# A second buffer for gathered expert rows, other groups of routed blocks, and one weight buffer less

## The chip, the cores and the metric

The kernel runs on one core of a Trainium2 chip. The metric is the device time of one execution in microseconds. TensorE is called PE here, its weight loads PEld, VectorE DVE, ScalarE ACT, GpSimd POOL and SyncE SP, as in the profile; SP only issues DMAs.

## What is computed

One layer of a decoder trunk on 1024 tokens of width 1024: a mixer (three kinds of token mixing side by side and one output projection), then a mixture of 32 experts, of which each token uses two, and a last RMSNorm.

```python
x = x + g_m * hybrid_mixer(h, w_in, ..., w_out)
h = rms_norm(x, norm_ffn_g) * (1.0 + sc_f) + sh_f
p_g = softmax(h @ w_rg + b_rg)                 # 4 groups, the best one is taken
e_logits = (h @ w_re + b_re)[chosen group]     # 8 experts in it, the best two
hid = silu(xb @ w_gate[e]) * (xb @ w_up[e])    # per expert, on the rows sent to it
out = out + (hid @ w_down[e]) * weight         # back to the tokens' rows
return rms_norm(x + g_f * out, final_norm_g)
```

## The kernel before

Tokens lie in 8 blocks of 128. The mixer ends in `c_steps(b, ...)`, block by block: eight groups of three products of `w_out` for each half of the columns (`ps_wo`, L990 to L992; each fp32 operand is split into a high and a low part, hence three), the residual sum `xb` on DVE (L996), its squares on ACT, and its store to `x1_d`. What follows for block b is spread between the products of block b+1: `post_steps` turns `xb` on PE (`ps_x1t`), multiplies it by the router's weights (`ps_rt`, L1016), writes the logits `L[:, b]` (L1021, L1022), and makes `h2`, the normalised rows that the experts read, which are stored to `h2_d` (L1033). For blocks 0 to 6 `h2` is one multiplication on DVE (L1025) and an addition of `shf` that DVE and POOL share (L1028), and ACT issues the store. For block 7 a multiplication by `af` (L1011) stands early on DVE, ACT multiplies by the row's factor (L1031), POOL adds `shf` (L1032) and SP issues the store.

`route_steps(b0, b1)` works on the logits of several blocks at once, as `RB` says: blocks 0 to 3 behind block 3, 4 to 6 behind block 6, and 7 alone at the end. It picks group and experts on DVE by some 30 small instructions, counts positions with PE (`ps_pos`, L1109 to L1112), and puts the token numbers and the weights into tables of 128 rows by 32 experts with PE (`ps_tab`, L1130 and L1166), two products a block each. The last group's table, `toki` (L1138), tells which 128 rows each expert takes.

The experts run one after another. `gather(e)` (L1306) is an indirect DMA from POOL's queue that reads the rows of expert e from `h2_d` into the one buffer `xg`. `xpose(e)` turns them on PE (`ps_xg`, L1316), eight transposes of 128 by 128 into two PSUM banks, and splits them into `xh` and `xl`. `next_tokens(e)` calls `xpose(e)` and then `gather(e + 1)`, inside the second product of the expert before. Then come the gate and up products (`ps_gu`, L1338 to L1340), the hidden rows, and the down products (`ps_d`), whose weighted result is added to `x1_d` by an indirect DMA from POOL (L1376, called the scatter).

An expert's weights are 6 MB, loaded by SP in halves of 1 MB (`load_half`, L1197) into a ring of `NHALF` = 19 buffers, made of whatever room the mixer leaves free as it ends: `w0`, the pair of `xq0` and the room of `gm` (`wg`), `xq1`, `cy`, and at last the room of `w_out`'s parts (`wx`). Sixteen of them are loaded ahead; the last `POST` = 3 wait until three small memsets on POOL (L1383), which stand behind the first gather, have run. A load may be issued when the load `DC` = 2 places ahead of it has landed, for the first `NC_` = 12, and `DEPTH` = 5 places ahead after that. ACT copies each piece of weights to the high part (`phi`, L1326), DVE subtracts to get the low part (`plo`, same line).

A scheduler sets each engine's order when the program is built, by its own estimates of time; at run time each engine works in that order and waits where data or room is missing. POOL's indirect DMAs stand in POOL's order like its instructions. At the end the last expert's rows are handled apart, with `xr`, which reuses `xg`.

Of the kernel before, what the change touches and what calls it, by code (L numbers as in the profile page):

```python
# [29 lines left out]
DE = 512  # L30
NOV = 15
NSSD = 2
NHALF = 19
SB = 3
XK, HK = 1, 3
WARM = 25
# [6 lines left out]
CP = 11  # L43
AN = 4
QD = 1
DC, NC_ = 2, 12
KORD = (4, 5, 6, 7, 0, 1, 2, 3)
RATE = 1.8
ZW = 2
# [1 line left out]
DEPTH = 5  # L51
NEG = -1.0e30

RB = {3: (0, 4), 6: (4, 7), 7: (7, 8)}


C_BSH, C_BSC, C_NMG = 0, 8, 16
# [17 lines left out]
def mixer_moe(ctx, tc, x, pch, prow, ada_m, ada_r, w_col, w_z, w_v, w_dtf, w_out, w_rt, w_gu, w_dn, out):  # L75
# [902 lines left out]
    def c_steps(b, yh, yl, xbs):  # L978
        bs = slice(b * P, (b + 1) * P)
        xb = xin[b]  # L980
        xT = sc3.tile([P, KT, P], F32, tag="xT", name="xT")
        s2 = sc.tile([P, 4], F32, tag="s2", name="s2")
        h2 = sc3.tile([P, D], F32, tag="h2", name="h2")
        for q in range(2):
            qs_ = slice(512 * q, 512 * (q + 1))
            ps = bank("ps_wo", "pj")
            for n, kt in enumerate(KORD):
                hi, lo = (woc[k][q][:, kt] for k in ("hi", "lo"))
                h_, l_ = (y[:, kt // 4, kt % 4] for y in (yh, yl))
                PE.matmul(ps, h_, hi, start=(n == 0), stop=False)  # L990
                PE.matmul(ps, l_, hi, start=False, stop=False)
                PE.matmul(ps, h_, lo, start=False, stop=(n == KT - 1))  # L992
                if q and n == 5:
                    turn(xb, xT, 0)
                yield
            V.tensor_tensor(xb[:, qs_], ps, xb[:, qs_], op=ALU.add)  # L996
            S.activation(ps, xb[:, qs_], AF.Square, accum_out=s2[:, q:q + 1])
        s1 = S.dma_start(x1_d[bs, :], xb)
        if b == XB:
            room(xsp.tile([P, 4096], F32, name="w0"), s1.ins)  # L1000
            room_of(xqs[0], woc["gmp"].tile([P, D], F32, tag="gm", name="wg"), after=s1.ins)
            room_of(xqs[1], xqs[2], xqs_both, after=s1.ins)
        xbs.append((xb, xT, s2, h2))

    def post_steps(b, xb, xT, s2, h2):
        bs = slice(b * P, (b + 1) * P)
        turn(xb, xT, 1)
        V.tensor_tensor(s2[:, 2:3], s2[:, 0:1], s2[:, 1:2], op=ALU.add)
        rstd_of(s2[:, 3:4], s2[:, 2:3], D, sc, 1)
        if b == NB - 1:  # L1010
            tc.keep_in_program_order(V.tensor_tensor(h2, xb, ccn["af"], op=ALU.mult))  # L1011
        yield
        yield
        pr = bank("ps_rt")
        for kt in range(KT):
            PE.matmul(pr[64 * (kt % 2):64 * (kt % 2) + 64, 0:P], ccn["wrp"][:, kt], xT[:, kt], start=(kt < 2), stop=(kt >= KT - 2))  # L1016
        rT = sc3.tile([P, P], F32, tag="rT", name="rT")
        rc = S.copy(rT, pr[:, 0:P])
        yield
        PE.transpose(pr[:, P:2 * P], rT, ident)  # L1020
        V.scalar_tensor_tensor(L[:, b], pr[:, P:P + 36], s2[:, 3:4], ccn["rbias"], op0=ALU.mult, op1=ALU.add)  # L1021
        V.scalar_tensor_tensor(L[:, b], pr[:, P + 64:P + 100], s2[:, 3:4], L[:, b], op0=ALU.mult, op1=ALU.add)  # L1022
        yield
        if b < NB - 1:
            V.scalar_tensor_tensor(h2, xb, s2[:, 3:4], ccn["af"], op0=ALU.mult, op1=ALU.mult)  # L1025
            for q in range(2):
                hs = slice(512 * q, 512 * (q + 1))
                (V if q else G).tensor_tensor(h2[:, hs], h2[:, hs], ccn["shf"][:, hs], op=ALU.add)  # L1028
        else:
            with tc.issue_after(rc.ins):  # L1030
                S.mul(h2, h2, s2[:, 3:4])  # L1031
            G.tensor_tensor(h2, h2, ccn["shf"], op=ALU.add)  # L1032
        (S if b < NB - 1 else nc.sync).dma_start(h2_d[bs, :], h2)  # L1033
        if b + 2 < NB:
            load_x1(b + 2, S)

# [188 lines left out]
    for b in range(NB):  # L1225
        c = b + NSSD
        ssd = ssd_steps(c, yns, **cst) if c < NB else iter(())
        if c >= NB and ew is None:
# [1 line left out]
            ew = ews.enter_context(tc.tile_pool(name="ew", bufs=1, side="right", reuse_waits="tile"))  # L1230
            room(ew.tile([P, 4096], F32, name="w1"))
            room(ew.tile([P, 2048], F32, name="w2"))
            xg = ew.tile([P, D], F32, name="xg")
            G.memset(xg, 0.0)
        yh, yl = nxt
        for n, _ in enumerate(c_steps(b, yh, yl, xbs)):
            next(ssd, None)
# [65 lines left out]

    with tc.tile_pool(name="ex", bufs=2, reuse_waits="tile") as ex:
        def gather(e):
            return G.indirect_dma_start(xg[:, :], None, h2_d[:, :],  # L1306
                                 bass.IndirectOffsetOnAxis(ap=toki[:, e:e + 1], axis=0),
                                 bounds_check=T - 1, oob_is_err=False)

        def xpose(e):  # L1310
            xh = ex.tile([P, KT, P], F32R, tag="xh", name="xh", bufs=1)
            xl = ex.tile([P, KT, P], F32R, tag="xl", name="xl", bufs=1)
            for q in range(2):
                pt = bank("ps_xg")
                for j in range(4):
                    PE.transpose(pt[:, j * P:(j + 1) * P], xg[:, (4 * q + j) * P:(4 * q + j + 1) * P], ident)  # L1316
                split(xh[:, 4 * q:4 * q + 4], xl[:, 4 * q:4 * q + 4], pt.rearrange("p (j c) -> p j c", c=P))
            return xh, xl

# [61 lines left out]
        with tc.issue_after(g1.ins):  # L1381
            for h in halves[NHALF - POST:]:
                G.memset(h[0][:, 0:1], 0.0)  # L1383
        for _ in range(POST):
            load_half()

# [12 lines left out]
        def next_tokens(e):  # L1399
            if e < NE:  # L1400
                xt.append(xpose(e))
                if e + 1 < NE:
                    gather(e + 1)

        xt, hts = [], []
        next_tokens(0)
# [34 lines left out]
        xbs = free[4:]  # L1441
        for b in LORD:
            nc.sync.dma_start(xbs[b], x1_d[b * P:(b + 1) * P, :])
        xr, XE = xg, G
        rows_of = bass.IndirectOffsetOnAxis(ap=toki[:, NE - 1:NE], axis=0)
        nf = FB * P
        G.indirect_dma_start(xr[:, :], None, x1_d[0:nf, :], rows_of, bounds_check=nf - 1, oob_is_err=False)
# [188 lines left out]
```

## Time and profile before

| what | us |
|---|---|
| median of three runs | 1296.21 |
| lowest and highest of them | 1293.31, 1296.91 |
| the profiled execution | 1301.8 |
| its span, first to last instruction | 1299.9 |
| PE busy | 1202.9 (93%) |
| DVE busy | 976.7 (75%) |
| ACT busy | 738.4 (57%) |
| POOL busy | 270.6 (21%) |

All stages and durations below are those of the profiled execution, whose time lies 5.6 us above the median. The mixer reaches from 0 to about 640 us of its span, the experts from about 655 to 1265, and the last norm ends it. Busy shares are averages over stages with different limits, so they are read for one stage at a time. A row of the order of time has the start, the duration, engine, line, operation, what is written and read, and in brackets the engine's idle time before it and what ended it.

### The profile page before, as it was taken

To read this page: it belongs to the slowest core of one execution; us is meant where nothing else is said; L and a number is where in the kernel's file an instruction comes from. 1 tells how busy PE (TensorE), PEld (TensorE's weight loads), DVE (VectorE), ACT (ScalarE), POOL (GpSimd) and SP (SyncE) were. 2 spreads that over 40 slices of the span, in tenths; PEclk is the share of its full clock that TensorE was granted. 3 is DMA by queue.
4 is the path that set the end of the run, shared out by engine and by line. 5 is a ranking of instruction groups with operands and counts; after the bars stand their busy time and mean duration, and the time that the engine had idled before them with its cause. 6 is when DMAs were issued, how large, how long until landed. Compare 5 with 4: busy or idle time off the path is not lost. (4 is left out here: it accounts for less than half of the span.)

```text
span 1299.9 us, 17279 instructions
## 1 busy us (share of the span) xinstructions
PE 1202.9 (93%) x6079; PEld 930.8 (72%) x6079; DVE 976.7 (75%) x1384; ACT 738.4 (57%) x1146; POOL 270.6 (21%) x200
## 2 busy tenths in 40 slices
PE   5999989999999879999789899999999999999993
PEld 4676646867677558778577677778777877787772
DVE  4789961145265676565678888999999999999985
ACT  4323312233354656653257676777777777787763
POOL 3110302300100253432112222221222122211113
PEclk9999989999999979999879999999999999999997
DMA  9315658642301453734979999999999999999726
GB/s 360 131 42 162 205 166 270 165 114 68 110 17 45 138 171 98 272 109 171 363 267 328 322 321 336 329 364 366 362 359 368 358 364 363 370 359 377 244 53 251
DMA packets 94635, 313.21 MB, mean 241 GB/s; under 512 B 24038, under 2 KB 34454, under 8 KB 73424
## 3 DMA queue, kind: packets, MB, share of 16 engines
q1 hardware_dynamic: 62190, 256.77, 54.3%
q10 hardware_dynamic: 14098, 31.99, 7.2%
q0 software_dynamic: 18256, 23.30, 7.2%
q8 instruction: 49, 0.80, 0.2%
q14 instruction: 42, 0.34, 0.1%
HBM read 289.22 MB, written 39.88 MB: 253 GB/s over the span
## 5 line engine op out<-in xcount | busy, mean ns | idle before, releaser
L1340 PE MATMUL ps_gu<-plo,xh 128*128 128x512 f32 x512 | 209.8, 410 | 7.9 <-DVE plo L1326 7.9
L1338 PE MATMUL ps_gu<-phi,xh 128*128 128x512 f32 x512 | 204.6, 400 | 0.0
L1339 PE MATMUL ps_gu<-phi,xl 128*128 128x512 f32 x512 | 201.8, 394 | 0.6 <-DVE xl L128 0.6
L1326 ACT CAST phi<-wx 128x1024 fp32r<-128x1024 f32 x160 | 167.4, 1053 | 61.6 <-PE ps_gu L1339 55.1
L1326 DVE TENSOR_TENSOR plo<-wx,phi 128x1024 fp32r<-128x1024 f32 x160 | 191.4, 1221 | 14.1 <-ACT phi L1326 9.9
L1376 POOL DMA_INDIRECT x_d<-early,toki x31 | 76.2, 2457 | 378.8 <-DVE early L1372 374.7
L1326 DVE TENSOR_TENSOR plo<-w,phi 128x1024 fp32r<-128x1024 f32 x104 | 125.2, 1221 | 10.8 <-ACT phi L1326 7.9
L1326 ACT CAST phi<-w 128x1024 fp32r<-128x1024 f32 x104 | 108.6, 1052 | 37.3 <-PE ps_gu L1339 32.9
L1340 PEld LDWEIGHTS ps_gu<-plo,xh 128*128 128x128 f32 x512 | 97.1, 190 | 38.0 <-DVE plo L1326 18.5
L1339 PEld LDWEIGHTS ps_gu<-phi,xl 128*128 128x128 f32 x512 | 97.3, 190 | 21.1 <-DVE xl L128 1.4
L1338 PEld LDWEIGHTS ps_gu<-phi,xh 128*128 128x128 f32 x512 | 97.2, 190 | 18.9 <-ACT xh L127 0.4
L1366 PE MATMUL ps_d<-phi,hh 128*128 128x512 f32 x256 | 100.8, 395 | 0.7 <-ACT hh L127 0.7
L1367 PE MATMUL ps_d<-phi,hl 128*128 128x512 f32 x256 | 100.4, 392 | 0.0
L1368 PE MATMUL ps_d<-plo,hh 128*128 128x512 f32 x256 | 96.6, 392 | 0.0
L182 PE MATMUL ps_pr<-h_hi,whi 128*128 128x512 f32 x224 | 91.7, 409 | 0.0
L184 PE MATMUL ps_pr<-h_hi,wlo 128*128 128x512 f32 x224 | 89.2, 398 | 1.3 <-POOL wlo L128 1.3
L183 PE MATMUL ps_pr<-h_lo,whi 128*128 128x512 f32 x224 | 89.3, 398 | 0.0
L223 DVE SCALAR_TENSOR_TENSOR cy<-u_t,cmw,cy 128x1024 f32<-128x1024 f32 x60 | 86.8, 1446 | 2.3 <-ACT cy L220 1.4
L128 POOL TENSOR_TENSOR wlo<-wraw,whi 128x1024 fp32r<-128x1024 f32 x14 | 38.3, 2748 | 178.8 <-ACT whi L127 124.6
L1306 POOL DMA_INDIRECT xg<-h_d,toki x32 | 38.6, 1208 | 109.1 <-PE ps_xg L1316 94.3
L990 PE MATMUL ps_wo<-wo_hi,yh 128*128 128x512 f32 x128 | 55.0, 432 | 1.5 <-ACT yh L127 1.5
L1366 PEld LDWEIGHTS ps_d<-phi,hh 128*128 128x128 f32 x256 | 48.3, 189 | 10.8 <-ACT hh L127 0.9
(403 smaller groups left out, 2629.4 us busy)
## 6 DMA issues: line engine op xcount, KB each, us to landing
wx<-in_w_gu_dram SPq DMA_DIRECT2D x53, 1024.0 KB, 11.6
w<-in_w_gu_dram SPq DMA_DIRECT2D x31, 1024.0 KB, 9.9
wx<-in_w_dn_dram SPq DMA_DIRECT2D x24, 1024.0 KB, 11.7
w<-in_w_dn_dram SPq DMA_DIRECT2D x19, 1024.0 KB, 10.9
at<-in_ada_r_dram ACTq DMA_DIRECT2D x64, 256.0 KB, 4.8
cy<-in_w_gu_dram SPq DMA_DIRECT2D x14, 1024.0 KB, 5.3
wy<-in_w_gu_dram SPq DMA_DIRECT2D x28, 512.0 KB, 13.8
wraw<-in_w_col_dram SPq DMA_DIRECT2D x16, 512.0 KB, 6.0
```

The source lines that it names most:

```text
L182: PE.matmul(ps, hi[:, kt, :], h_hi[hf][:, kt, :], start=(kt == 0), stop=False)
L183: PE.matmul(ps, hi[:, kt, :], h_lo[hf][:, kt, :], start=False, stop=False)
L184: PE.matmul(ps, lo[:, kt, :], h_hi[hf][:, kt, :], start=False, stop=(kt == KT - 1))
L223: yield lambda t=t, k=k: V.scalar_tensor_tensor(cy[:, :, t], v128(u_t[:, t, k:k + T]), cmw[:, t, k:k + 1], cy[:, :, t], op0=ALU.mult, op1= ...
L1326: last[:] = [S.copy(hi, raw).ins, V.tensor_tensor(lo, raw, hi.bitcast(F32), op=ALU.subtract).ins]
L1338: PE.matmul(ps, xh[:, kt], hi[:, ks], start=(kt == 0), stop=False)
L1339: PE.matmul(ps, xl[:, kt], hi[:, ks], start=False, stop=False)
L1340: PE.matmul(ps, xh[:, kt], lo[:, ks], start=False, stop=(kt == KT - 1))
L1366: PE.matmul(pd[n], hh[:, f], hi[:, ns], start=(f == 0), stop=False)
L1367: PE.matmul(pd[n], hl[:, f], hi[:, ns], start=False, stop=False)
L1368: PE.matmul(pd[n], hh[:, f], lo[:, ns], start=False, stop=(f == 3))
L1376: G.indirect_dma_start(x1_d[:, :], bass.IndirectOffsetOnAxis(ap=toki[:, e:e + 1], axis=0), yo[:, :], None, bounds_check=T - 1, oob_is_err= ...
```

## The change

`xq0` becomes the second buffer for gathered rows: `xgs` holds `xg` and `xq0`, expert e uses `xgs[e % 2]`, and both are set to zero once. `gather(1)` is issued right behind the three memsets, and `next_tokens(e)` issues `gather(e + 2)` where it issued `gather(e + 1)`. The pair of `xq0` and the room of `gm` leaves the ring of weight buffers, which has 18 halves then, 15 of them loaded ahead, all 15 two at a time. The routed groups are blocks 0 to 3, 4 and 5, and 6 and 7. The last block's `h2` gets its factor and `shf` in one DVE instruction, and ACT issues its store.

```diff
-NHALF = 19
+NHALF = 18
-DC, NC_ = 2, 12
+DC, NC_ = 2, 15
-RB = {3: (0, 4), 6: (4, 7), 7: (7, 8)}
+RB = {3: (0, 4), 5: (4, 6), 7: (6, 8)}
...
             room(xsp.tile([P, 4096], F32, name="w0"), s1.ins)
-            room_of(xqs[0], woc["gmp"].tile([P, D], F32, tag="gm", name="wg"), after=s1.ins)
             room_of(xqs[1], xqs[2], xqs_both, after=s1.ins)
...
-            with tc.issue_after(rc.ins):
-                S.mul(h2, h2, s2[:, 3:4])
-            G.tensor_tensor(h2, h2, ccn["shf"], op=ALU.add)
-        (S if b < NB - 1 else nc.sync).dma_start(h2_d[bs, :], h2)
+            V.scalar_tensor_tensor(h2, h2, s2[:, 3:4], ccn["shf"], op0=ALU.mult, op1=ALU.add)
+        S.dma_start(h2_d[bs, :], h2)
...
-            xg = ew.tile([P, D], F32, name="xg")
-            G.memset(xg, 0.0)
+            xgs = [ew.tile([P, D], F32, name="xg"), xqs[0]]
+            for xg in xgs:
+                G.memset(xg, 0.0)
...
-            return G.indirect_dma_start(xg[:, :], None, h2_d[:, :],
+            return G.indirect_dma_start(xgs[e % 2][:, :], None, h2_d[:, :],
...
-                    PE.transpose(pt[:, j * P:(j + 1) * P], xg[:, (4 * q + j) * P:(4 * q + j + 1) * P], ident)
+                    PE.transpose(pt[:, j * P:(j + 1) * P], xgs[e % 2][:, (4 * q + j) * P:(4 * q + j + 1) * P], ident)
...
                 G.memset(h[0][:, 0:1], 0.0)
+        gather(1)
...
                 xt.append(xpose(e))
-                if e + 1 < NE:
-                    gather(e + 1)
+                if e + 2 < NE:
+                    gather(e + 2)
...
-        xr, XE = xg, G
+        xr, XE = xgs[0], G
```

The program's order at the end of the mixer, on PE: `ps_x1t` and `ps_rt` are the turned rows and the router's products of block 7, `ps_tab` the tables. Before, from the last products of `w_out` on:

```order
L1130 MATMUL ps_tab<-rEv_5532,rph_5530 128x32
L973 MATMUL ps_x1t<-ident,xb 128x128 x8
L1016 MATMUL ps_rt<-xT,wrp 64x128 x3
L1130 MATMUL ps_tab<-rEv_5542,rph_5540 128x32
...
L1016 MATMUL ps_rt<-xT,wrp 64x128
L1166 MATMUL ps_tab<-roh_5513,rph_5530 128x32
...
L1016 MATMUL ps_rt<-xT,wrp 64x128 x4
L1020 MATMUL ps_rt<-ident,rT 128x128
```

And the same place in the changed program:

```order
L992 MATMUL ps_wo<-wo_lo_3558,yh 128x512
L973 MATMUL ps_x1t<-ident,xb 128x128 x4
L1015 MATMUL ps_rt<-xT,wrp 64x128 x8
L1019 MATMUL ps_rt<-ident,rT 128x128
L1106 MATMUL ps_pos<-rohr,tri_ltr 128x64
```

The tables of the group before the last have left this place; they stand among the products of `w_out` for block 7 now.

The first expert on PE, `ps_gu` being its first gate product. Before:

```order
L1316 MATMUL ps_xg<-ident,xg 128x128 x8
L1338 MATMUL ps_gu<-phi,xh 128x512
L1339 MATMUL ps_gu<-phi,xl 128x512
L1340 MATMUL ps_gu<-plo,xh 128x512
L1338 MATMUL ps_gu<-phi,xh 128x512
```

Changed, with `xq_3931` the second buffer:

```order
L1314 MATMUL ps_xg<-ident,xg 128x128 x8
L1314 MATMUL ps_xg<-ident,xq_3931 128x128 x2
L1336 MATMUL ps_gu<-phi,xh 128x512
L1314 MATMUL ps_xg<-ident,xq_3931 128x128 x5
L1337 MATMUL ps_gu<-phi,xl 128x512
```

Two transposes of expert 1's rows stand ahead of expert 0's first product now, five more right behind it.

POOL's order from the first gather on (`h_d` is `h2_d`, `x_d` is `x1_d`). Before:

```order
L1306 DMA xg<-h_d,toki 128x1024
L1383 MEMSET wx 128x1 x2
L1383 MEMSET wy 128x1
L1306 DMA xg<-h_d,toki 128x1024 x3
L1376 DMA x_d<-early,toki 1024x1024
L1306 DMA xg<-h_d,toki 128x1024
```

Changed:

```order
L1304 DMA xg<-h_d,toki 128x1024
L1381 MEMSET wx 128x1 x2
L1381 MEMSET wy 128x1
L1304 DMA xq_3931<-h_d,toki 128x1024
L1304 DMA xg<-h_d,toki 128x1024
L1304 DMA xq_3931<-h_d,toki 128x1024
L1304 DMA xg<-h_d,toki 128x1024
L1374 DMA x_d<-early,toki 1024x1024
L1304 DMA xq_3931<-h_d,toki 128x1024
```

Five gathers stand ahead of the first scatter instead of four, into the two buffers in turn.

## Rows read from the trace of the kernel before

**Rows 1.** Stretches of the expert stage: length, busy time by engine, clock, DMA share, GB/s.

```profile
700.00:800.00 100.00, 90.76 (x423) 74.19 (x422) 88.86 (x90) 71.80 (x80) 21.16 (x10) 0.98 0.93 327
900.00:1200.00 300.00, 294.59 (x1366) 238.39 (x1365) 288.86 (x294) 231.78 (x262) 55.10 (x32) 1.00 0.99 365
655.00:1226.00 571.00, 549.83 (x2536) 445.36 (x2535) 532.29 (x544) 428.88 (x482) 108.64 (x65) 0.99 0.96 348
```

**Rows 2.** Order of time on POOL, three of the scatters (L1376).

```profile
694.96 3.47 POOL L1376 DMA_INDIRECT x_d<-early,toki  x1 [3.07 <-DVE early L1372]
...
818.54 2.32 POOL L1376 DMA_INDIRECT x_d<-early,toki  x1 [14.18 <-DVE early L1372]
...
1206.27 2.32 POOL L1376 DMA_INDIRECT x_d<-early,toki  x1 [14.70 <-DVE early L1372]
```

**Rows 3.** PE's waits in 660 to 830 us: total, times, longest.

```profile
PE ps_xg L1316 <- DMA xg<-h_d,toki: 12.2, 5, 3.3
```

**Rows 4.** Gathers: two in 653 to 662, seven in 670 to 800, 21 in 820 to 1200.

```profile
DMA to landing us min/median/max: 4.4/6.2/8.0
...
DMA to landing us min/median/max: 5.3/8.0/9.2
...
DMA to landing us min/median/max: 8.4/12.2/13.7
```

**Rows 5.** Two stretches behind waits; columns as in rows 1.

```profile
759.00:763.00 4.00, 3.76 (x12) 3.18 (x13) 1.51 (x3) 1.04 (x1) 0.95 (x1) 0.57 1.00 329
799.00:805.00 6.00, 5.80 (x23) 4.74 (x24) 2.23 (x2) 2.04 (x2) 1.28 (x1) 0.72 0.91 304
```

**Rows 6.** PE's waits in 830 to 1210 us.

```profile
PE ps_gu L1340 <- DVE plo L1326: 7.1, 21, 0.4
```

**Rows 7.** Order of time from the last products of `w_out` to the first gate product.

```profile
622.82 1.28 DVE L1025 SCALAR_TENSOR_TENSOR h<-xb,s,af 128x1024 f32<-128x1024 f32 x1 [0.67 <-POOL s L124]
...
632.53 0.40 PE L992 MATMUL ps_wo<-wo_lo,yh 128*128 128x512 f32 x1
...
633.65 0.47 PE L990 MATMUL ps_wo<-wo_hi,yh 128*128 128x512 f32 x1
...
634.19 0.40 PE L992 MATMUL ps_wo<-wo_lo,yh 128*128 128x512 f32 x1
...
638.91 2.02 PE L1166 MATMUL ps_tab<-roh,rph 128*128 128x32 f32 x12 [0.58 <-DVE tab L1134]
...
642.99 0.26 DVE L1021 SCALAR_TENSOR_TENSOR L<-ps_rt,s,rbias 128x36 f32<-128x36 f32 x1 [1.83 <-PE ps_rt L1020]
...
643.50 2.34 POOL L1032 TENSOR_TENSOR h<-h,shf 128x1024 f32<-128x1024 f32 x1 [4.33 <-ACT h L1031]
...
643.76 2.10 DVE L1077 TENSOR_TENSOR rc<-L,rm 128x4 f32<-128x4 f32 x1
...
645.87 0.33 SPq L1033 DMA_DIRECT2D h_d<-h  x1
...
653.46 0.18 DVE L1138 CAST toki<-tf 128x32 int32<-128x32 f32 x1
...
653.95 1.17 POOL L1306 DMA_INDIRECT xg<-h_d,toki  x1 [8.11 <-DVE toki L1138]
...
658.40 1.97 PE L1316 MATMUL ps_xg<-ident,xg 128*128 128x128 f32 x8 [0.59 <-DMA xg<-h_d,toki]
...
660.19 0.79 PE L1338 MATMUL ps_gu<-phi,xh 128*128 128x512 f32 x1
```

**Rows 8.** What SP's loads waited for: in 655 to 900, then in 900 to 1200 us.

```profile
SPq L1197 <- DVE plo L1326: 196.3, 82, 5.9
...
SPq L1197 <- DMA wx<-in_w_gu_dram: 57.3, 25, 4.5
```

**Rows 9.** The last loads on SP, and the last piece of weights read, on ACT.

```profile
1219.92 6.43 SPq L1197 DMA_DIRECT2D w<-in_w_dn_dram  x4
...
1266.61 1.04 ACT L1326 CAST phi<-w 128x1024 fp32r<-128x1024 f32 x1 [2.46 <-PE ps_d L1367]
```

## The prediction, before the changed kernel was run

> **What bounds the kernel now.** I read the stages first, then who PE waited for, then the order of time around each wait. Over the expert stage [rows 1] PE is busy 98% of the time from 900 to 1200 us, but only 90.8% from 700 to 800, where DVE and the DMA engines have room too. So the stage has a pace that PE sets, and a stretch ahead of it that does not reach this pace. The reader can check that pace in the scatters of the experts' results on GpSimd [rows 2]: from the one at 818.54 to the one at 1206.27 lie 21 experts, 18.46 us each; from 694.96 to 818.54 lie 6, 20.60 us each. The six lost 6 x 2.14 = 12.8 us.
>
> The waits name the cause: between 660 and 830 us PE waited five times, 12.2 us in all, for the gather of an expert's rows [rows 3]. Before has one buffer `xg`, so the gather for expert e+1 can't be issued before PE has turned the rows of expert e. Landing takes 5.3 to 9.2 us after the issue here, and 12.2 us in the median later, when no transpose waits for it [rows 4]. PE runs its instructions in order, so what is queued behind the waiting transposes, the expert's matmuls, waits too.
>
> Two of these waits have an echo: in 759 to 763 and in 799 to 805 us the granted clock was 0.57 and 0.72 [rows 5], between the levels of 1.2 and 2.4 GHz, right behind a wait. Lost: 4 x 0.43 + 6 x 0.28 = 3.4 us of PE time. Waits and clock make 15.6 us, yet the pace shows 12.8. The difference is there because DVE uses PE's waits to get ahead: PE's wait for `plo` is 7.1 us in 21 times once the gathers are in time [rows 6], 0.34 us an expert, which the early experts are spared. Removed waits give that back: 15.6 - 6 x 0.34 = 13.6.
>
> **Part 1, two buffers.** Gather e+2 is issued when the transposes of expert e are through, and its rows are wanted two experts later: 2 x 18.46 = 37 us, or, where PE's order takes the first transposes early, some 90 of PE's instructions at 294.59 / 1366 = 0.22 us [rows 1], 20 us. Either is more than the longest landing of 13.7 us [rows 4]. The five waits go, and the two dips of the clock behind them. Worth 12.8 by the pace, 13.6 by the other sum; I take 13.1. In GpSimd's queue the fifth gather stands ahead of the first scatter as the fourth did, both wait for the same transposes, and nobody new queues behind them. The memset of the second buffer stands far ahead in GpSimd's order and costs nothing there; were it late, so would be the first gather into that buffer.
>
> **Part 2, the way from the last products of w_out to the first gather.** Now: last product at 634.19, logits of block 7 on DVE at 642.99, token table at 653.46, gather at 653.95 [rows 7]. Three pieces move.
> (a) The routing of blocks 4 to 6 stood partly behind the last products. Now blocks 4 and 5 are routed among the first products of block 7, which PE runs without gaps today: 8 small products at 2.02 / 12 = 0.17 us, 1.3 us, and up to 1 us of waits of PE for DVE's masks. The group of position products that stood among the last ones goes (from 632.53 to 633.65, less the 0.23 of a product: 0.9 us). The last product comes 0.4 to 1.4 us later, I take 1.0.
> (b) Behind it, the twelve weight products (2.02 us at 638.91, and 0.58 of waiting before them) no longer stand ahead of the router's products of block 7. In exchange DVE does the whole second step of `h2` ahead of the logits, as one instruction like that of 1.28 us. This gains 1.3 to 2.6 us; I take 2.0, since DVE's step partly lies under PE's router products.
> (c) From the logits to the table 10.7 us go by. In them one DVE instruction on 4 elements took 2.10 us while GpSimd added `shf` (643.50, 2.34 us); its neighbour takes 0.26. That add is gone: -1.9. Two blocks at once instead of one cost wider instructions, two more sums ahead of the table and three more products: 0 to 2 us, I take 1.0.
> The Trainium skill, SBUF — State Buffer, § Who interferes with whom, says that a DVE instruction with two SBUF inputs and a GpSimd one that reads SBUF exclude each other for a whole instruction. The row at 643.76 agrees; if its 2.10 us had another cause, the sum under (c) would lack its 1.9, and the median would be 1285.
> Together, 1.0 - 2.0 - 0.9, the table comes 1.9 us earlier (bounds 0 and 4). The store of `h2` hides: issued at 645.87 now, at about 642 then, on ScalarE's queue behind the store of `x1`; with two loads in flight instead of five it has some 10 us until the gather. Were that cover gone, each us of its delay would be one of the gather.
>
> **Part 3, a new wait.** In PE's new order two transposes of expert 1 stand ahead of the first gate product. So PE's first product waits for the second gather. That one is issued 1.17 + 0.3 us after the first (that one's own time, and three memsets of one column at 0.1 each, my estimate from DVE's 0.26 us for 36 columns), when the loads that those memsets release start too. Before shows both ends: 4.4 us for the first gather, with the DMA engines idle, and 8.0 for the second, among loads [rows 4]. First gather at 653.95 - 1.9 = 652.05, second at 653.5, landed at 657.9 to 661.5; two transposes at the lower clock add 0.5 (eight took 1.97). The first product comes at 658.4 to 662.0 instead of 660.19 [rows 7]; I take 7 us for the landing, nearer to the second gather's: 661.0, 0.8 later. But the eight transposes, 1.0 us at full clock, are then nearly all done. Parts 2 and 3 together: about 0, from -3 to +1.
> The Trainium skill, DMA: Bandwidth & Descriptors, § Queues, rings and completion order, says that a DMA engine takes turns between its queues packet by packet. An estimate by it is at most twice the lone 4.4, so 8.8 us, and the first product at 662.8, by which the median would be 1285; the row of 8.0 lies within that.
>
> **Part 4, 18 buffers of weights instead of 19, and loads two at a time until the gather.** At 700 to 900 us the loads wait for free buffers (196.3 us on `plo` [rows 8]), not for the DMA engines. The last load is issued at 1226, and its last piece is read at 1266.61 [rows 9]: some 40 us, of which the landing takes at most about 14 if it is as slow as the slowest gather [rows 4]. PE comes 13 us earlier, and 13 us are left. The lost buffer matters only while buffers are what the loads wait for. Zero while this cover holds; its loss is the second rival. Two at a time costs nothing either: an expert's 6 MB last PE 18.46 us, so the last of 15 preloaded MB is read some 40 us after the first product.
>
> **The sum.** 13.1 + 0 off the profiled execution's 1301.8 us is 1288.7. That execution is 5.6 us above the median of 1296.2. If this excess is spread over the run, the median becomes 1283.1, my forecast **1283**. If all 5.6 lay in the waits for gathers, only 7.5 would be gained: 1288.7.
>
> **Rivals.**
> *The second gather comes late.* It meets a burst of loads and lands as slowly as the later ones, 12.2 us. First product at 666.2, 6.0 later, 1.0 given back: 1288. For it: the loads are released in the same moment. Against: 8.0 us is the nearest row.
> *The DMA engines become the bound.* This one ends slower. Before moves 348 GB/s on average from 655 to 1226 us [rows 1], and from 900 on the loads wait for loads (57.3 us for one group alone [rows 8]), at 365 GB/s and a busy share of 0.99: not much is left. With PE 13 us earlier the loads must be late by 13 + 13 = 26 us to cancel the gain, so it decides when the mean rate falls under 348 x 571 / 597 = 333 GB/s. The 327 of 700 to 800 us is such a rate. Held throughout, it makes the loads 37 us late: 1296.2 + 11 = 1307. Against it: 327 came while the loads waited for buffers, and 365 lasted 300 us.
> *The change doesn't do what it says.* If the gathers still stand behind something in GpSimd's queue, or PE's order asks for the rows earlier too, half of the waits stays: 1283 + 6.5 = 1289.5. For it: the order moves transposes of the next expert forward in several experts. Against it: over 20 us lie between issue and use in all of them.
>
> **Chances.** Forecast 0.74 (1276 to 1287); late second gather 0.10; waits partly stay 0.11; DMA the bound 0.05. The three runs of before lie within 3.6 us, so some 2 us either way are chance. The range of 8 in 10 reaches from 1276 (part 2 at its best, 3 us, the second sum of the waits, and chance) to 1290 (both rivals near 1289). A measurement can tell about 0.3%, 3.9 us, so faster means under 1292.3: 0.90, the forecast, the late gather and most of the waits that stay. Within: 0.06. Slower: 0.04.
>
> **What will show it.** Right: PE's waits for a gather between 660 and 830 us fall from five to none, the experts' pace is about 18.5 us from the first scatter on, the granted clock stays at 1.00 there. The table of tokens comes 0 to 3.5 us earlier, no DVE instruction of 2 us stands in the routing, and PE waits 1 to 4 us for the second gather. Wrong: waits of ScalarE's casts for loads, a pace over 19 us, or a wait for a gather after the second expert.

## The result, and the profile after

| | before | changed |
|---|---|---|
| median, us | 1296.56 (4 runs, 1293.31 to 1298.67) | 1285.58 (4 runs, 1285.37 to 1288.95) |
| profiled execution, us | 1301.8 | 1285.73 |
| its span, us | 1299.9 | 1283.9 |

The ratio of the times is 0.9918, with a 95% interval of 0.9894 to 0.9942: 11.0 us faster. The profiled execution of before lies 5.2 us above its median, that of the changed kernel on its own, so the two traces differ by more than the kernels: by 16.0 us of span, 1299.9 against 1283.9.

The stages first, as in [rows 1]: of the changed kernel the time of the stretch, PE, PEld, DVE, ACT and POOL busy, the granted clock, the share and the rate of the DMA engines.

```profile
700.00:800.00 100.00, 99.26 (x465) 81.14 (x465) 97.21 (x100) 79.63 (x91) 20.79 (x11) 1.00 0.98 365
900.00:1200.00 300.00, 294.67 (x1366) 238.41 (x1365) 288.89 (x292) 232.12 (x261) 53.78 (x31) 1.00 0.97 362
655.00:1226.00 571.00, 560.85 (x2594) 455.11 (x2594) 543.74 (x555) 440.92 (x496) 105.51 (x60) 0.99 0.95 351
```

The stretch from 700 to 800 us was at 90.76 and is at 99.26 of 100 us; from 900 on nothing has changed. The scatters on POOL, which answer to [rows 2], give the pace:

```profile
694.25 3.47 POOL L1374 DMA_INDIRECT x_d<-early,toki  x1 [4.21 <-DVE early L1370]
...
803.22 2.32 POOL L1374 DMA_INDIRECT x_d<-early,toki  x1 [14.70 <-DVE early L1370]
...
1190.95 2.31 POOL L1374 DMA_INDIRECT x_d<-early,toki  x1 [14.71 <-DVE early L1370]
```

Six experts from 694.25 to 803.22 are 18.16 us each (20.60 before), the 21 behind them 18.46, as before. The whole of what PE waited for from 660 to 830 us, in total, times and longest, against the five waits and 12.2 us of [rows 3]:

```profile
PE ps_gu L1338 <- DVE plo L1324: 1.7, 5, 0.4
PE ps_gu L1336 <- ACT xh L127: 1.4, 1, 1.4
```

No gather is among them. Ahead of the first gate product the picture is another one. PE in order of time, as in [rows 7]:

```profile
645.58 1.91 PE L1163 MATMUL ps_tab<-roh,rph 128*128 128x32 f32 x8
652.88 3.75 PE L1278 MATMUL ps_row<-sl,ident 8*128 8x128 f32 x16 [5.38 <-DMA sl<-g_rows]
656.56 1.97 PE L1314 MATMUL ps_xg<-ident,xg 128*128 128x128 f32 x8
658.32 0.64 PE L1314 MATMUL ps_xg<-ident,xq 128*128 128x128 f32 x2
658.60 0.78 PE L1336 MATMUL ps_gu<-phi,xh 128*128 128x512 f32 x1
```

POOL's order beside it, with the two gathers (`xq` is the second buffer, and the memsets that release loads stand between):

```profile
646.58 1.17 POOL L1304 DMA_INDIRECT xg<-h_d,toki  x1 [11.20 <-DVE toki L1135]
...
648.09 1.71 POOL L1304 DMA_INDIRECT xq<-h_d,toki  x1 [0.16 <-issue]
```

The first landed after 7.3 us (4.4 before), as the transfers of `xg` in that stretch show:

```profile
DMA to landing us min/median/max: 7.3/7.3/7.3
```

The table was ready and the first gather issued at 646.58, 7.4 us earlier than before; the first gate product comes at 658.60, only 1.6 earlier, and the first scatter 0.7 earlier. In between PE waits 5.38 us for `sl`, a row of 4 KB (the gate `g_f` of the experts' result, spread over the partitions by `ps_row`) that SP loads. What the reader is to take from these rows: the gain lies in the loop, and most of the 7.4 microseconds by which the first gather stands earlier have gone again before the loop begins. Some 3.4 of the 7.4 can't be put down to the change, as the next section shows.

### The profile page after: what moved, and what is told of

Its sections match the earlier page's. It is cut to its first block, busy times and chain, and to the rows that moved or that the text cites. A ratio compares the mean times of both kernels' runs of the same rounds, so it can differ in the third digit from the quotient of the medians.

```text
span 1283.9 us, 17260 instructions
## 1 busy us (share of the span) xinstructions
PE 1195.3 (93%) x6079; PEld 927.3 (72%) x6079; DVE 973.4 (76%) x1386; ACT 736.4 (57%) x1145; POOL 266.0 (21%) x200
## 5 line engine op out<-in xcount | busy, mean ns | idle before, releaser
L1324 DVE TENSOR_TENSOR plo<-wx,phi 128x1024 fp32r<-128x1024 f32 x166 | 198.1, 1220 | 7.1 <-ACT phi L1324 4.4
L1324 ACT CAST phi<-wx 128x1024 fp32r<-128x1024 f32 x166 | 173.1, 1055 | 50.0 <-PE ps_gu L1337 41.5
L1324 ACT CAST phi<-w 128x1024 fp32r<-128x1024 f32 x110 | 115.3, 1050 | 59.9 <-PE ps_gu L1337 53.2
L1324 DVE TENSOR_TENSOR plo<-w,phi 128x1024 fp32r<-128x1024 f32 x110 | 130.8, 1220 | 7.4 <-ACT phi L1324 6.1
L1324 DVE TENSOR_TENSOR plo<-cy,phi 128x1024 fp32r<-128x1024 f32 x44 | 53.7, 1221 | 6.0 <-ACT phi L1324 4.9
L1364 PEld LDWEIGHTS ps_d<-phi,hh 128*128 128x128 f32 x256 | 48.0, 188 | 10.8 <-ACT hh L127 0.9
## 6 DMA issues: line engine op xcount, KB each, us to landing
wx<-in_w_dn_dram SPq DMA_DIRECT2D x30, 1024.0 KB, 14.4
```

Source lines behind the costliest of these rows:

```text
L1324: last[:] = [S.copy(hi, raw).ins, V.tensor_tensor(lo, raw, hi.bitcast(F32), op=ALU.subtract).ins]
L1364: PE.matmul(pd[n], hh[:, f], hi[:, ns], start=(f == 0), stop=False)
```

## Where the 16 us of the two traces lie

The last store of `x1` ends the mixer. Measured from it, a stretch can be compared between executions whose mixers took different times:

| us | before | changed | difference |
|---|---|---|---|
| start to last store of `x1` | 636.1 | 632.7 | -3.4 |
| last store to table of tokens | 17.4 | 13.4 | -4.0 |
| last store to first gate product | 24.1 | 25.9 | +1.8 |
| last store to first scatter | 58.9 | 61.5 | +2.6 |
| first to 28th scatter | 511.3 | 496.7 | -14.6 |
| 28th scatter to the end | 93.6 | 92.9 | -0.7 |

The rows on the last store, the first scatter, the 27 experts and the end make -16.1, the 16.0 of the spans within rounding. The first of them, -3.4, can't be put down to the change: in the fourteen profiled kernels of this study the last store of `x1` stands between 631.4 and 637.2 us, and kernels that share the old routing stand at both sides (636.1 for before, 631.8 with 18 buffers). The granted clock of the mixer differs between these traces too (0.88 to 0.93 from 400 to 500 us); how much of the difference that makes was not worked out. What is left, -2.6 + 14.6 + 0.7, is 12.7 us of gain, by the trace.

## Experiments

Each kernel was timed beside the kernel before, whose median was 1295.2 to 1297.4 in these comparisons. Times are in us; the ratio is to before, with its 95% interval; the last four columns are of the profiled execution.

| kernel | median (lowest, highest) | ratio | table | gate | scatter | pace |
|---|---|---|---|---|---|---|
| before | 1296.56 | 1 | 17.4 | 24.1 | 58.9 | 20.60 |
| changed | 1285.58 (1285.37, 1288.95) | 0.9918 [0.9894, 0.9942] | 13.4 | 25.9 | 61.5 | 18.16 |
| e_two_bufs | 1286.46 (1284.4, 1288.05) | 0.9928 [0.9907, 0.9948] | 16.4 | 27.8 | 63.6 | 18.17 |
| e_one_buf | 1295.37 (1292.24, 1298.97) | 1.0001 [0.9984, 1.0019] | 13.4 | 25.1 | 59.0 | 19.70 |
| e_route_h2 | 1296.2 (1290.5, 1300.9) | 1.0006 [0.9984, 1.0028] | 13.3 | 24.0 | 58.4 | 20.50 |
| e_ring18 | 1295.75 (1292.94, 1299.92) | 0.9996 [0.9981, 1.0010] | 16.4 | 23.1 | 58.0 | 20.60 |
| e_ring14 | 1287.5 (1285.56, 1292.01) | 0.9933 [0.9910, 0.9955] | 13.4 | 20.2 | 60.2 | 18.38 |
| e_nc12 | 1286.72 (1284.46, 1288.03) | 0.9931 [0.9911, 0.9951] | 13.4 | 26.4 | 61.3 | 18.15 |
| e_sl_act | 1286.71 (1281.23, 1288.0) | 0.9922 [0.9898, 0.9945] | 13.4 | 24.5 | 62.2 | 18.37 |
| e_g2_sl | 1286.44 (1284.73, 1287.51) | 0.9919 [0.9899, 0.9939] | 13.3 | 24.1 | 61.0 | 18.37 |
| e_warm | 1283.25 (1280.98, 1288.03) | 0.9894 [0.9873, 0.9915] | 13.4 | 27.4 | 62.3 | 18.17 |
| e_late | 1285.49 (1280.35, 1290.55) | 0.9922 [0.9896, 0.9947] | 13.4 | 21.1 | 55.2 | 18.36 |
| e_warm_late | 1284.47 (1283.47, 1286.59) | 0.9912 [0.9894, 0.9930] | 13.4 | 24.5 | 58.0 | 18.37 |
| e_best | 1285.81 (1284.15, 1287.61) | 0.9923 [0.9905, 0.9941] | 13.3 | 23.7 | 57.2 | 18.37 |

Table, gate and scatter are counted from the last store of `x1`; the pace is that of the first six experts.

### Which part carries the gain

**e_two_bufs**: before with the second buffer alone.

```diff
-NHALF = 19
+NHALF = 18
...
+            xgs = [ew.tile([P, D], F32, name="xg"), xqs[0]]
...
+        gather(1)
```

> The kernel before with the second buffer for gathered rows alone (and the 18 buffers of weights that this leaves); routing groups, the way of h2 and the pace of the preloads are as before. My theory: the gain is that of the waits for gathers and of the clock behind them, and parts 2 and 3 cancel, so this kernel lies within 1.5 us of the changed one: 1284 to 1287, no wait of PE for a gather between 675 and 830 us, first six experts 18.0 to 18.5 us each. Rival, the earlier table of tokens is worth its 7 us less the new wait: this kernel lies 2 us or more above the changed one, 1288 to 1292, with the same pace.

**e_one_buf**: the changed kernel with one buffer for rows and the old two gather calls again, but 18 buffers of weights.

> The changed kernel with one buffer for gathered rows, as before (gather of the next expert behind the transposes of this one), all else as changed, 18 buffers of weights too. My theory: the waits for gathers are back, 3 to 6 of them and 8 to 15 us in all between 660 and 830 us, and with them nearly the whole time: 1293 to 1298. Rival, the routing groups and the shorter way to the table carry several us on their own: 1287 to 1291.

The second buffer alone gives 0.9928, everything else without it 1.0001. In the second kernel PE's waits from 660 to 830 us begin with

```profile
PE ps_xg L1313 <- DMA xg<-h_d,toki: 8.3, 3, 3.5
```

and the pace is 19.70. So the theory held for both, and by the medians the buffer is the gain. The trace of e_one_buf doesn't say quite as much: three waits of 8.3 us stand there, not five of 12.2, and its first six experts take 5.4 us less than those of before. Its median shows nothing of this, and with an interval of 0.9984 to 1.0019 it could hide at most some 2 us of gain; whether its other runs wait as little is not known. The rival for the first, that the earlier table is worth several microseconds, falls: a table 3 us later (16.4 for 13.4) costs 0.9 us in the medians, less than they can tell.

In the first kernel Part 3's mechanism stands in the open. PE's waits from 640 to 700 us begin with:

```profile
PE ps_pos L1108 <- DVE rEv L1121: 7.1, 1, 7.1
PE ps_xg L1316 <- DMA xq<-h_d,toki: 4.3, 1, 4.3
```

`xq` is the second buffer: the first gate product stands behind two transposes of expert 1, and its gather took 9.2 us to land. The first gate product comes 27.8 us behind the last store of `x1`, against 23.1 with the same routing and one buffer (e_ring18).

**e_route_h2**: before with the routing groups and the way of `h2` alone.

```diff
-RB = {3: (0, 4), 6: (4, 7), 7: (7, 8)}
+RB = {3: (0, 4), 5: (4, 6), 7: (6, 8)}
...
+            V.scalar_tensor_tensor(h2, h2, s2[:, 3:4], ccn["shf"], op0=ALU.mult, op1=ALU.add)
+        S.dma_start(h2_d[bs, :], h2)
```

> The kernel before with part 2 alone: routing groups of 4, 2 and 2 blocks, the second step of h2 in one DVE instruction, its last store on ScalarE's queue. One buffer for rows, 19 buffers of weights and preloads 0 to 11 two at a time, as before. Measured from the last store of x1, the kernel with 18 buffers and the old routing had the table at 16.4 us and the first gate product at 23.1; with the new routing and 15 preloads two at a time 13.4 and 25.1. Theory A, the pace of the preloads lost what the routing won: here the table comes at 13.4 and the first gate product at 19.5 to 21.5, and 1292 to 1295. Theory B, whatever brings the table forward meets loads in flight, and the first gather lands 3 us later instead: table 13.4, gate 23 to 25.5, and 1294.5 to 1297.5.

1.0006: nothing. The table comes at 13.3, 3.0 earlier than in e_ring18, and the first gate product at 24.0, 0.9 later. That is Theory B: with 12 preloads at two a time as well the first gather, issued earlier, meets loads in flight, and lands after 8.0 us instead of 4.4. Five waits for gathers, 11.6 us, stand in the loop as before.

**e_ring18**: before with `NHALF` 18 and without the pair of `xq0` and `wg`.

> The kernel before with 18 buffers of weights instead of 19 and nothing else (what the second buffer for rows takes from the weights, without the second buffer). Part 4 of the prediction, the lost buffer costs nothing because some 13 us of cover are left behind the last load: within 2 us of the kernel before, 1294 to 1297. Rival, the buffer is worth something that the second gather buffer pays back: 1298 to 1303, and the second buffer alone would then be worth more than 9 us.

0.9996, with waits for gathers that have the number and the total of [rows 3] (the longest is 2.6, there 3.3):

```profile
PE ps_xg L1315 <- DMA xg<-h_d,toki: 12.2, 5, 2.6
```

The lost buffer costs nothing. The run tells one thing more: its profiled execution took 1295.49 us, with the same waits and the same pace of 20.60 as that of before at 1301.8. The excess of the latter over its median was not in the waits. The first scatter stands at 689.80 here and at 694.96 there: 5.2 of the 6.2 us between the spans lie ahead of the loop.

**e_ring14**: the changed kernel with `NHALF` 14. Here the rows of the last norm share buffers with the last weights, so what is computed behind the last expert is another thing, and only what lies ahead of it is read.

> The changed kernel with 14 buffers of weights instead of 18, so 11 MB are loaded ahead of the experts, not 15. Part 4's cover of 13 us: four MB less loaded ahead are 4 x 1.05 MB at 365 GB/s, 11.5 us more of loads behind the first gather, so the loads end just in time: 0 to 3 us slower than the changed kernel, 1285 to 1289. Rival, the cover is smaller than worked out, because the DMA engines are busy 0.97 of the stage already: 8 us slower or more, 1293 to 1298, with waits of ScalarE's casts for loads.

The pace is 18.38 and then 18.48 us an expert, and no wait of ACT or PE for a load reaches 0.7 us between 655 and 1226 us; the first theory holds. The rate of the loads over that stage:

```profile
655.00:1226.00 571.00, 556.95 (x2569) 449.74 (x2568) 539.88 (x551) 435.76 (x490) 103.71 (x59) 0.99 0.97 356
```

356 GB/s, more than the changed kernel moved (351), so the DMA engines had something left. A side of it: with the loads ahead of the experts done early (a DMA share of 0.24 from 640 to 655 us) the first gather landed after 4.5 us and the first gate product came 20.2 us behind the last store of `x1`, the earliest of all. Little was won by it: the second gather still took 9.2 us, PE waited 3.8 us for it inside the first products, and the first scatter stands at 60.2.

### What the first product waits for

The changed kernel shows a wait for `sl`, which stands on SP's queue behind preloads:

```profile
645.47 0.33 SPq L1194 DMA_DIRECT2D wx<-in_w_dn_dram  x1
645.85 0.32 SPq L1272 DMA_DIRECT2D sl<-g_rows  x1
```

**e_nc12** sets `NC_` back to 12, **e_sl_act** moves the row to ACT's queue:

```diff
-    def row_load(src, dst):
-        nc.sync.dma_start(dst, src.rearrange("(a b) -> a b", b=P))
+    def row_load(src, dst, q=None):
+        (q or nc.sync).dma_start(dst, src.rearrange("(a b) -> a b", b=P))
...
-row_load(g_rows[0, 3072:4096], sl[0:8, :])
+row_load(g_rows[0, 3072:4096], sl[0:8, :], S)
```

> The changed kernel, the preloads 12 to 14 five at a time as before instead of two at a time; the instructions of every engine and their order are the same. Theory A, PE's new wait of 5.38 us for the 4 KB row sl comes from the place of its transfer on SP's queue behind preloads that go two at a time, and the second gather (landed at 657.68) stands right behind it: sl is issued some 3 to 6 us earlier, its wait shrinks under 2 us, PE waits for the second gather instead and the first gate product comes only 0 to 1 us earlier, 1284 to 1286. Theory B, that wait is the bound of the transition: first gate product 2 to 3 us earlier, 1281.5 to 1283.5. Theory C, five loads in flight slow the gathers: first product later than 659.5, 1286.5 or more.

> The changed kernel with the 4 KB row sl loaded on ScalarE's queue, not on SP's; the scheduler now also puts the first gate product ahead of the transposes of expert 1 and four of these right behind it. Theory A, behind the wait for sl the second gather is next: the wait for sl goes (under 1 us left), one for the second gather of 1 to 4 us comes, first products 0 to 1.5 us earlier, 1284 to 1286. Theory B, sl alone was the bound: no wait for the second gather, first gate product 2 to 3 us earlier, 1281.5 to 1283.5. If the wait stays, it does not come from SP's queue.

PE's waits for transfers from 640 to 700 us in the first and then in the second:

```profile
PE ps_xg L1314 <- DMA xg<-h_d,toki: 2.7, 1, 2.7
PE ps_row L1278 <- DMA sl<-g_rows: 1.8, 1, 1.8
...
PE ps_xg L1314 <- DMA xq<-h_d,toki: 1.2, 1, 1.2
```

```profile
PE ps_xg L1314 <- DMA xg<-h_d,toki: 4.3, 1, 4.3
...
PE ps_xg L1314 <- DMA xq<-h_d,toki: 1.1, 1, 1.1
```

Theory A held in both in its waits, and more of it than expected: behind the wait for `sl` stands one for the first gather, behind that one for the second. 5.4 us of one wait became 5.7 of three, or 5.4 of two, and both medians are within 1.2 us of the changed kernel, 0.7 above the range of Theory A, which is less than they can tell. The first gate product of e_nc12 came 0.5 us later, not 0 to 1 earlier. For Theory C the trace decides nothing: with five loads in flight the first gather of e_nc12 landed after 9.0 us, 7.3 in the changed kernel, but with two it took 8.7 in e_sl_act. In e_nc12 `sl` was issued at 634.69, eleven microseconds earlier, and PE still waited for it until 648.93. These 14.2 us are no less than a load of 1 MB takes: 11.0 to 14.4 us in the median from issue to landing, by groups of loads of the changed kernel.

**e_g2_sl** adds the second gather straight behind the first, ahead of the memsets.

```diff
-        g1 = gather(0)
+        gather(0)
+        g1 = gather(1)
         with tc.issue_after(g1.ins):
...
-        gather(1)
```

> The changed kernel with the row sl on ScalarE's queue, and with the second gather issued straight behind the first, ahead of the three memsets that release loads (in the changed kernel it stands behind them). Theory A, the first product waits for both gathers, and they land late because of loads in flight that were issued before (0.94 of the DMA engines busy from 640 to 650): the second gather lands 0 to 1.5 us earlier, first gate product 656.5 to 658.5, median 1284 to 1287, no difference that can be told. Theory B, the loads that the memsets release slow the second gather: it lands 3 us or more earlier, no wait of PE for it, 1281 to 1283.5.

The second gather landed after 10.3 us, hardly sooner (10.8 in e_sl_act, 9.6 in the changed kernel); PE waited 3.9 us for the first and 0.8 for the second. Theory A again: the loads that the memsets release are not what delays the second gather. That the loads issued before the gathers do fits e_best, below, where fewer of them are in flight: 4.3 and 7.1 us.

**e_late** is e_g2_sl with the transposes of expert 1 behind the gate products of expert 0; `mms` collects the last of each three of these products.

```diff
-                    PE.matmul(ps, xh[:, kt], lo[:, ks], start=False, stop=(kt == KT - 1))
+                    mms.append(PE.matmul(ps, xh[:, kt], lo[:, ks], start=False, stop=(kt == KT - 1)).ins)
...
-                    next_tokens(1)
+                    with tc.issue_after(mms[7]):
+                        next_tokens(1)
```

> As the kernel with sl on ScalarE's queue and the second gather straight behind the first, and in PE's order the transposes of expert 1 now stand behind all 24 gate products of expert 0 (there two to four stood ahead of the second product). Theory, the second gather is a term of its own: its wait of 0.79 to 1.06 us and the clock that stays at 0.50 behind it (to 662 to 665) cost 2 to 3 us; without it the first scatter comes 57.5 to 60 us after the last store of x1 (61.0 with it) and the median is 1283 to 1285. Rival, the wait only moves (to ScalarE's casts or to the transposes), the same scatter and 1286 to 1287.

PE's way into the first products:

```profile
653.94 1.94 PE L1314 MATMUL ps_xg<-ident,xg 128*128 128x128 f32 x8 [0.87 <-DMA xg<-h_d,toki]
655.70 0.79 PE L1336 MATMUL ps_gu<-phi,xh 128*128 128x512 f32 x1
```

and the clock behind them:

```profile
658.00:661.00 3.00, 3.00 (x15) 2.47 (x14) 2.37 (x6) 2.18 (x3) 0.00 (x0) 1.00 0.99 410
```

In e_two_bufs, where the wait of 4.3 us stands ahead of the first product, the clock was still at 0.50 later than that:

```profile
661.00:664.00 3.00, 3.00 (x9) 2.32 (x9) 0.07 (x1) 1.04 (x1) 0.00 (x0) 0.50 0.17 68
```

In the trace the term is there: PE waits 0.87 us, for the first gather alone, and the first scatter comes at 55.2, 5.9 earlier than in e_g2_sl. Only half of that belongs to the moved transposes. 3.0 us lie ahead of the first gate product (21.1 for 24.1), where the first gather landed after 5.4 us instead of 8.4, with the DMA engines as busy (0.95 from 640 to 654 us, 0.97 there); nothing in the edit touches it, and why it was faster is open. Behind the first gate product 2.9 us are left, within the 2 to 3 that were expected. The median, 1285.49, doesn't show it; its six runs lie between 1280.35 and 1290.55, and the profiled one, at 1282.15, is the second fastest of them. So the theory holds for the trace, and the worth of it in time stays open.

**e_warm** and **e_warm_late** add ten products of the identity between `ps_row` and the first transposes, to e_g2_sl and to e_late.

```diff
+        pw = bank("ps_warm")
+        with tc.issue_after(g1.ins):
+            for _ in range(10):
+                PE.matmul(pw[:, 0:P], ident, ident, start=True, stop=True)
```

> As the kernel with sl on ScalarE's queue and the second gather straight behind the first, and ten products of the identity (their result isn't used) between the row products and the transposes of the first gather, so that PE has no idle time there while it waits for the rows. Theory, an idle PE ahead of the first products keeps the clock at 0.50 for 3.6 to 7 us into them (after a wait of 1.06 us it came back to 1.00 at 664.7, without one at 660.1): the clock is at 1.00 by 657 to 661, 2 to 3 us are gained against the kernel without these products, 1282 to 1284.5. Rival, the gathers bound the first products anyway and the clock comes back no earlier: within 1 us of the kernel without them.

> As the last kernel, and ten products of the identity (not used for the output) between the row products and the transposes of the first gather. Theory, the clock is then at 1.00 from 656 to 659 on, with no second wait that takes it away again: first scatter 56 to 58.5 us after the last store of x1, 1 to 2 us faster than the kernel without the ten, 1281 to 1283.5. Rival, the ten products themselves delay the transposes of the first gather as much as the clock gives back: within 1 us.

The clock of e_warm ahead of the first products, and behind them:

```profile
650.00:655.00 5.00, 5.00 (x26) 4.77 (x24) 2.69 (x7) 0.65 (x2) 0.00 (x0) 0.55 0.90 289
656.00:660.00 4.00, 1.16 (x9) 0.98 (x10) 1.29 (x2) 1.07 (x2) 0.99 (x1) 1.00 1.01 422
662.00:664.00 2.00, 2.00 (x6) 1.56 (x5) 0.34 (x1) 1.04 (x1) 0.00 (x0) 0.50 0.89 359
```

With PE busy the clock came to 1.00 ahead of the products, as expected. Then PE waited 1.41 us for the first gather and 2.25 us for the second, and the clock fell to 0.50 just as the gate products ran. The median of 1283.25 is the lowest of all, and within what the theory gave, but its interval overlaps those of the changed kernel and of e_g2_sl (0.9899 to 0.9939). Its trace shows no earlier scatter (62.3), but it is that of its slowest run, 1288.03; what the faster five did is not shown. In e_warm_late there is no second wait, and the clock stays; the scatter, 58.0, is later than without the ten (55.2). That is the rival in part only: of the 3.4 us by which the first gate product comes later, 2.0 are the first gather's, which landed after 7.4 us instead of 5.4, and some 1.5 the ten products', behind which the transposes start at 656.19, not at the landing at 654.6. From the first gate product to the first scatter 0.6 us are given back. The two medians, 1284.47 and 1285.49, can't be told apart.

**e_best** is e_warm_late with six buffers loaded only behind the gathers (`POST` = 6).

> As the kernel with the ten products, and six buffers instead of three are loaded only behind the gathers, so that the loads ahead of the table end earlier and the DMA engines are nearly idle when the gathers are issued (with 14 buffers they were 0.24 busy from 640 to 655, and the first gate product came 20.2 us after the last store of x1, against 25.9 in the changed kernel). Theory, the landing of the first gather falls from 7.3 us to 4.3 to 5 and the first gate product to 20 to 22 us after the last store of x1; 2 to 3 us on top, 1279 to 1282. Rival, PE still has row products and the ten to do until about 655, or the 3 MB loaded later (3 x 1.05 MB at 365 GB/s, 8.6 us) are missed at the end: no gain, or a loss, against the kernel with three.

The first gather landed after 4.3 us, as the theory says, at 652.1; but `ps_row` and the ten products stand ahead of its transposes, which began at 656.39. So the theory had the landing right and the rest wrong: the first gate product came at 23.7, not at 20 to 22, and 1285.81 is not faster than e_warm_late. That is the first half of the rival. The same without the ten products was not tried.

## Why the prediction was right, and where it was not

**Part 1, two buffers** (13.1 us): right in its mechanism and nearly in size. The waits and the dips of the clock behind them are gone, the trace gives 14.6, and the medians of e_two_bufs and e_one_buf show that the buffer is the gain. The term was 1.5 too small: both sums took the later pace of 18.46, or the give-back to DVE, as the floor of the early experts, but these now run at 18.16, and the first three of them at 17.84 to 17.88. Most of the 1.5 seems to be borrowed from ahead of the loop. The four kernels in which PE waits 1.4 us for `xh` before the first scatter (changed, e_two_bufs, e_nc12, e_warm) have a pace of 18.15 to 18.17, the six others with two buffers, which lack this wait, 18.36 to 18.38, so 13.4 us for the six experts. That fits the give-back to DVE that the prediction named; no run shows it by itself.

**Part 2, the way to the table** (1.9 us earlier, 0 to 4): right for the table, 3.0 to 4.0 earlier by the last store of `x1`, where (b) and (c) had 2.9. The 1.0 us of (a) lies ahead of that store and can't be told from the scatter of its times. The DVE instruction of 2.10 us [rows 7] is gone. In e_ring18, which has the old way of `h2`, it stands again and ends with POOL's addition:

```profile
638.40 2.24 DVE L1076 TENSOR_TENSOR rc<-L,rm 128x4 f32<-128x4 f32 x1
```

```profile
638.28 2.34 POOL L1031 TENSOR_TENSOR h<-h,shf 128x1024 f32<-128x1024 f32 x1 [3.37 <-ACT h L1030]
```

638.40 + 2.24 and 638.28 + 2.34 are the same moment within 0.02 us, and in the changed kernel, without the addition, the same instruction, for two blocks then, takes 0.17 us. By the rule of the Trainium skill, SBUF — State Buffer, § Who interferes with whom, a DVE instruction with two SBUF inputs and a GpSimd one that reads SBUF shut each other out for a whole instruction; the trace agrees.

**Part 3, the new wait, and parts 2 and 3 together** (about 0, from -3 to +1): this is the step that failed. Measured from the last store of `x1` the first scatter came 2.6 us later, outside of that range. The wait for the second gather was named, and e_two_bufs shows it bare, at 4.3 us: against e_ring18, which has one buffer and else the same, the first product comes 4.7 us later and the first scatter 5.7, where the prediction's sum, without the 1.9 us of the earlier table, has 2.7 for the product. The second gather took 9.2 to 11.3 us in eight of the ten kernels that issue two (8.4 in e_late, 7.1 in e_best), not the 7 that was taken. The prediction's estimate by the Trainium skill, DMA: Bandwidth & Descriptors, § Queues, rings and completion order, had 8.8 at most; these eight went past it. What was overlooked is that a table which comes earlier puts the *first* gather among the loads as well. Before, the DMA engines had paused when it was issued (a share of 0.03 from 650 to 652 us and 0.00 from 652 to 654); now they are busy at 0.93 from 640 to 654 us (0.65 before), and it lands after 7.3 us. Of the 4.0 us of the earlier table 2.9 went there. The next 2.6 went to `ps_row`, which was not foreseen at all. Before, its products ran while the first gather landed, and waited for nothing:

```profile
654.03 3.78 PE L1280 MATMUL ps_row<-sl,ident 8*128 8x128 f32 x16
```

Now they wait 5.38 us for `sl`, start at 652.88, and hold PE until the transposes at 656.56, though the first gather landed at 653.9. Counted from the last store of `x1` the landing is 1.1 us earlier than before, the start of the transposes 1.5 later, the first gate product 1.8 later, with two transposes of expert 1 ahead of it, and the first scatter 2.6 later. In the last step lie five more of these transposes and a wait of PE of 1.39 us for `xh`, behind which the granted clock is 0.50 once more from 674 to 676 us; how they share it was not told apart.

**Part 4, 18 buffers and loads two at a time** (nothing): right for the buffer, which e_ring18 shows alone, and for the cover, of which e_ring14 takes 4 MB, 11.5 us, without a wait. "Two at a time costs nothing" was right in its result and not in its reason: SP's queue was held by these loads, `sl` landed behind them, and PE waited 5.38 us. It costs nothing because two gathers were waited for behind it, as e_nc12 shows.

**The sum.** 13.1 + 0 was 14.6 - 2.6 + 0.7 in the trace, 12.7 for 13.1. The terms were off by 1.5 and 0.7 one way and by 2.6 the other: that the total came this close is luck. The excess of the profiled run was either spread (1283.1) or in the waits (1288.7); by e_ring18 it lay ahead of the loop. 1296.2 - 12.7 is 1283.5, and 1285.58 was measured; 2 us are no more than the runs of one kernel differ by, and what they are is open.

**The rivals.** The late second gather is real as a mechanism, and cheaper than the rival had it: the rival took 12.2 us for the landing, which is 7.1 to 11.3 in ten kernels, and 7.9 us for the first product where the table is not earlier, which is 4.7 in e_two_bufs. In the changed kernel PE never waited for it: it landed after 9.6 us, at 657.7, while PE was at what stood behind the wait for `sl`, and the transposes that need it began at 658.32. The DMA engines did not become the bound: 351 GB/s, and 365 where 327 had been. That the gathers would still wait was wrong: none is waited for behind the first products.

## What to carry to other kernels

A step ahead of a loop that is made faster starts its transfers earlier: look at what the DMA engines do at the new moment, not at the old one, before its gain is counted. Where several transfers are awaited one behind another, the trace names only the one that came last for each instruction, and taking it away shows the next; here the first product came much earlier (20.2 and 21.1 us behind the store, for 25.9) only where the first gather itself landed sooner, after 4.5 and 5.4 us, not where one wait was taken away. And a second buffer is priced by the pace of the loop with and without the wait, which here held to 1.5 us of 13.

## What was not expected of the hardware

A transfer of 4 KB behind loads of 1 MB on the same queue took 7.0 us (issued 645.85, PE's wait ended 652.88) in the changed kernel, 14.2 in e_nc12 (634.69 to 648.93) and 15.1 in e_route_h2 (635.22 to 650.32). On ACT's queue, in e_sl_act, it was issued at 640.44 and nobody waited for it when its products began at 647.3.

The first gather of 128 rows took 4.3 to 4.5 us in the five kernels where the DMA engines were 0.19 to 0.65 busy from 640 to 654 us (before, e_two_bufs, e_ring18, e_ring14, e_best), and 5.4 to 9.5 in the nine where they were 0.90 to 0.97 busy (5.4 in e_late, 6.3 in e_one_buf, 7.3 and more in the others). The second of two issued 1.5 to 1.6 us apart took 7.1 to 11.3. What sets the time within these ranges is open.
